# State-space scratch buffers in the form of the tiles, one transfer per unit for input, taps and output

## The chip, the cores and the metric

The kernel runs on one core of one Trainium2 chip. The metric is the time of one execution in microseconds of the device. The kernel before takes 2274.19 us, the median of three runs (2266.21 to 2277.70). Everything is float32; the large products are made of three matmuls each on a high and a low part.

## The reference

One layer of a hybrid encoder trunk: a projection whose columns go to a state-space branch (512 channels) and to chunked attention (8 heads of 64), both joined by one output projection, then a SwiGLU feed-forward. The state-space branch is the part that the change touches (SEQ 2048, 32 groups of 16 channels, 64 complex states per group):

```python
def s5_mixer(u, lam_re, lam_im, log_dt, b_re, b_im, c_re, c_im, d_skip, w_glu, b_glu):
    uf = u.astype(f32).reshape(bsz, seq, N_SSM_GROUPS, SSM_GROUP)
    ...
    lam_bar = jnp.exp(lam * dt)
    b_bar = ((lam_bar - 1.0) / lam)[..., None] * b_mat
    bu = jnp.einsum('bsgh,gph->bsgp', uf.astype(jnp.complex64), b_bar)
    ...
    _, states = lax.associative_scan(combine, (a, bu), axis=1)
    y = jnp.einsum('bsgp,ghp->bsgh', states, c_mat).real + d_skip.astype(f32) * uf
    y = jax.nn.gelu(y.reshape(bsz, seq, D_SSM))
    y = y * jax.nn.sigmoid(y @ w_glu.astype(f32) + b_glu.astype(f32))
    return y.astype(u.dtype)

def reference(...):
    h = rmsnorm(x, norm_mix_g[l]); proj = h @ w_in[l]
    ...
    mixed = jnp.concatenate([rmsnorm(y_ssm, ...), rmsnorm(y_att, ...)], axis=-1)
    x = x + mixed @ w_out[l]
    h2 = rmsnorm(x, norm_ffn_g[l])
    x = x + (jax.nn.silu(h2 @ w_gate[l]) * (h2 @ w_up[l])) @ w_down[l]
    return rmsnorm(x, norm_final_g)
```

## The kernel before

The program has five stretches, told here by the times of the profiled execution. From 0 to about 120 us `u_phase` makes the state-space input u for four blocks of 512 tokens, while `ssm_prologue` makes the taps and matrices of the scan and puts them into scratch buffers in memory. From 120 to about 700 us `att_phase` runs: 128 attention steps (4 blocks, 4 head pairs, 2 heads, 4 query blocks), each with scores, transposes and the product with v; between them stand units of other work, advanced step by step by class `Unit`: the projections of q, k and v of the next block (`qk_unit`, `v_unit`, `hT_unit`), and for the state-space branch eight times a `ssm_front` and a `ssm_back`. From about 700 to 960 us `mix_phase` makes the gated unit and the output projection; its first part is drawn into the last attention steps. Then come gate and up (960 to 1810 us) and down (to the end).

The state-space sequence is cut into pieces of L = 8 steps. A unit b handles GB = 4 groups: its input tile U has 128 partitions, which are 8 steps j times 16 channels c, and in each 4 groups times 256 pieces. So a row of the tile is 1024 numbers. Three scratch buffers in memory feed and empty these tiles:

- `S["u"]` is [512 channels, 4 blocks, 8 steps, 64]. `evac` (L484) writes it from the GpSimd queue, 16 times a [128, 512] tile, in rows of 2 KB. `ssm_front` reads it with eight DMAs per unit (L558 and L559, one for each step j, 16 partitions, runs of 64 numbers or 256 B).
- `S["kt"]` is [16, 32 groups, 2, 128]: zeros followed by the taps. `ssm_back` cuts eight shifted windows out of it, one DMA for each (L636 and L637, 16 partitions, runs of 512 B), into the tile Tm.
- `S["y"]` is [512 channels, 8 steps, 256]. `ssm_back` writes it with eight DMAs per unit (L650 and L651, runs of 1 KB). `fetch` (L1033) in the mix stage reads it back, twice 4 DMAs of 512 KB.

Channels of the group index and the channel within the group are in the order (c g) in u and in the order (g c) in y; the host lays the columns of the input projection out for the first.

All of these loads and the store of y go out on the queue of SyncE (SP), which issues in program order and waits in that order. The same queue carries the weights (`w<-wss`, 1 MB each), the bias rows of each head (`nba<-nbs` and `nbb<-nbs`, L549 and L550, one pair for each head), the copies of q between partition halves (`q2h`, `q2l`, L784 and L785), the keys (`ks`, L756 and L790) and the input of the next block (`xt` and `raw` from `in_xt`, L722). The DMAs of SP share eight completion semaphores in turn, so that each one waits for the one eight before it.

Which instruction stands where on a queue is decided by a scheduler when the program is built, except for TensorE, whose order is that of the text (`Ordered`, `PINA`), and a few marked instructions, among them the loads of unit 0 (the `b == 0` in `load`). GpSimd (POOL) also runs the scan of each unit (L592 to L604) and the moves of the carried states (`XG`, L626).

```python
SSM_F = 1 + GP + 7 + 7 + 3 + 4 + 1
SSM_B = 1 + GP + 1
SX = 4, 24, 35, 48, 61, 74, 87, 100
SY = 20, 36, 49, 62, 75, 88, 101, 114
```

SX and SY are the attention steps at which front and back of unit b begin.

Of the kernel before, what the change touches and what calls it, by code (L numbers as in the profile page):

```python
# [397 lines left out]
def u_phase(k, ident, S, aw):  # L398
# [3 lines left out]
    with ExitStack() as cx:  # L402
# [78 lines left out]
        def evac(b, f, ps):  # L481
            us = k.t(p3, "us", [P, L, NC // NSB])
            nc.vector.tensor_tensor(us[:], (jc if b else cj)(ps[:]), pbs[b], op=ALU.mult)
            nc.gpsimd.dma_start(S["u"][f * P : (f + 1) * P, b], us[:])  # L484

# [66 lines left out]


def ssm_front(k, p, psum, S, b, eng):

    nc = k.nc

    def load(out, in_):  # L558
        ins = nc.sync.dma_start(out, in_)  # L559
        if b == 0:  # L560
            k.tc.keep_in_program_order(ins)

    U = S["rsn"][:, : GB * NC].rearrange("p (g c) -> p g c", g=GB) if b and b % 2 == 0 else k.t(p, "U", [P, GB, NC])[:]
    k.U[b] = U
    for j in range(L):
        load(U[j * CH : (j + 1) * CH].rearrange("c g (n t) -> c g n t", n=NSB), S["u"].rearrange("(c g) n j t -> c g n j t", c=CH)[:, GB * b : GB * b + GB, :, j])
    bst = k.t(p, "Bst", [P, GB, P])
# [62 lines left out]
def ssm_back(k, p, psum, S, b):  # L630

    nc = k.nc
    F = GB * CH
    gs = slice(GB * b, GB * b + GB)
    tm = k.t(p, "Tm", [P, GB, P])
    for i in range(L):  # L636
        nc.sync.dma_start(tm[i * CH : (i + 1) * CH], S["kt"].rearrange("c g a m -> c g (a m)")[:, gs, P - CH * i : 2 * P - CH * i])  # L637
# [12 lines left out]
    for j in range(L):  # L650
        nc.sync.dma_start(S["y"][b * F : (b + 1) * F, j, :].rearrange("(g c) t -> c g t", c=CH), U[j * CH : (j + 1) * CH])  # L651
    yield


SSM_F = 1 + GP + 7 + 7 + 3 + 4 + 1
SSM_B = 1 + GP + 1
SX = 4, 24, 35, 48, 61, 74, 87, 100
SY = 20, 36, 49, 62, 75, 88, 101, 114
# [24 lines left out]
def att_phase(k, ident, S, aw, x0, roots):  # L683

    tc, nc, io, pfs = k.tc, k.nc, k.io, k.pfs
    with ExitStack() as cx:
# [253 lines left out]
        for sb in range(NSB):  # L940
# [7 lines left out]
            for gen, n, c in ((qk_unit(sb, 1), QK_N, 2), (qk_unit(sb, 2), QK_N, 3), (v_unit(sb, 1), V_N, 4), (qk_unit(sb, 3), QK_N, 5)):  # L948
                units.append(Unit(gen, n, g0 + C[c], g0 + C[c + 1], 2, light=LIGHT) if sb else Unit(gen, n + 1, C[c], C[c + 1], 4, light=LIGHT, mid=2))
        k.U = {}  # L950
        for b in range(NG // GB):
            units.append(Unit(ssm_front(k, sp, psum, S, b, k.ssm_eng), SSM_F, SX[b], SX[b] + 9, SX[b] - 2 if b == 0 else 2 if b == 1 else 5, light=SL))
            units.append(Unit(ssm_back(k, sp, psum, S, b), SSM_B, SY[b], SY[b] + 2, 6, light=SL))
# [27 lines left out]
def mix_phase(k, S, bank):  # L981
# [3 lines left out]
    with ExitStack() as cx:  # L985
# [44 lines left out]
        def fetch(sb):  # L1030
            yrs[0] = k.t(my, "yr", [P, 4, L, 128])
            for f in range(4):
                nc.sync.dma_start(yrs[0][:, f], S["y"][f * P : (f + 1) * P, :, sb * 64 : sb * 64 + 128])  # L1033

# [587 lines left out]
def block_kernel(tc, io, phases="pusamf"):  # L1622
# [3 lines left out]
    with ExitStack() as cx:  # L1626
# [4 lines left out]
        def pp():  # L1631
            return tc.tile_pool(name="psum", bufs=4, space=bass.MemoryType.PSUM, reuse_waits="tile")

        S = {
            "u": k.t(dram, "u", [DS, NSB, L, NC // NSB]), "y": k.t(dram, "y", [DS, L, NC]),
            "ya": k.t(dram, "ya_s", [NSB, DS, SB]), "x1": k.t(dram, "x1", [D, SEQ]),
# [3 lines left out]
            "hq": k.t(dram, "hq", [2, F2, 7, P, 512]), "wc": k.t(dram, "wc", [F2, 7, P, 512]), "wt": k.t(dram, "wt", [4, P, HALF]),  # L1640
            "kt": k.t(dram, "kts", [CH, NG, 2, P]),
        }
# [35 lines left out]
def layout(inputs):  # L1678
# [7 lines left out]
    def cols(v):  # L1686
        return np.ascontiguousarray(v.reshape(-1, P).T)

    def blocks(v, r, c):

        v = v.reshape(v.shape[0] // r, r // P, P, -1, c).transpose(0, 3, 2, 1, 4)
        return v.reshape(-1, P, r // P * c)

    x = a["x"][0].copy()
    x[SB:] = x[SB:].reshape(-1, SB // L, L, D).transpose(0, 2, 1, 3).reshape(-1, D)
    r = {
        "x": x, "xt": a["x"][0].T, "xp": x.T, "w_u": a["w_in"][0][:, :DS].reshape(D, NG, CH).transpose(0, 2, 1).reshape(D, DS),
        "w_qk": blocks(a["w_in"][0][:, DS : 3 * DS], D, P), "w_v": blocks(a["w_in"][0][:, 3 * DS :], D // 2, 256), "w_glu": a["ssm_w_glu"][0], "w_out": a["w_out"][0],
        "w_gate": blocks(a["w_gate"][0], D, P), "w_up": blocks(a["w_up"][0], D, P), "w_down": a["w_down"][0],
        "g_mix": cols(a["norm_mix_g"][0]), "g_ffn": cols(a["norm_ffn_g"][0]), "g_final": cols(a["norm_final_g"]),  # L1700
        "g_ssm": cols(a["norm_ssm_out_g"][0]), "g_att": cols(a["norm_att_out_g"][0]), "b_glu": cols(a["ssm_b_glu"][0]),
        "lam_re": pairs(a["ssm_lam_re"][0])[:, :, 0], "lam_im": pairs(a["ssm_lam_im"][0])[:, :, 0],
# [25 lines left out]
```

## Time and profile before

| what | value |
|---|---|
| median of three runs | 2274.19 us |
| the profiled execution, its own time | 2277.4 us |
| its span | 2275.6 us |
| TensorE matmul busy, share of the span | 2169.8 us, 95% |
| VectorE busy | 1542.7 us, 68% |
| ScalarE busy | 1002.5 us, 44% |
| GpSimd busy | 350.1 us, 15% |
| share of the 16 DMA engines taken by SP's queue | 54.6% |
| share taken by GpSimd's queue | 3.3% |
| mean granted TensorE clock | 0.978 |

The profile is one execution, followed instruction by instruction. Busy times of engines overlap, so they do not add up to the span. What matters for a change is the idle time of the engine that sets the end, here TensorE (PE), and what each of its waits was released by. The time of the profiled execution lies 3.2 us above the median.

### The profile page before, as it was taken

How to read it: one execution, taken by the hardware profiler on the slowest of the kernel's cores; microseconds unless marked ns; L12 is line 12 of the kernel's file. 1: busy time of each engine (PE TensorE's matmuls, PEld its weight loads, DVE VectorE, ACT ScalarE, POOL GpSimd, SP SyncE). 2: the span in 40 equal slices, each digit the busy share in tenths (PEclk: the TensorE clock that was granted, in tenths of full speed). 3: DMA queues.
4: the chain of work that ended last, by engine and by line, in shares of the span. 5: the costliest groups of instructions: out<-in, count | busy, mean ns of one | idle time of the engine just before them, and what ended most of it. 6: DMA issues, size and time to landing. Idle time of an engine off the chain costs nothing.

```text
span 2275.6 us, 30307 instructions
## 1 busy us (share of the span) xinstructions
PE 2169.8 (95%) x10632; PEld 1828.5 (80%) x10632; DVE 1542.7 (68%) x2695; ACT 1002.5 (44%) x1656; POOL 350.1 (15%) x827
## 2 busy tenths in 40 slices
PE   8989898999997899999999999999999999999997
PEld 6778787888986688878888887888888777888886
DVE  7757556555556756776767678666666477688776
ACT  6446555455557452343333335333333443353322
POOL 2246666646520000000000000000000010000000
PEclk9999999999998899999999999999999999999999
DMA  8778875766653535854555467655433395465652
GB/s 296 234 250 263 220 195 172 220 197 185 177 166 105 172 118 160 270 179 144 178 183 193 163 213 259 196 175 185 143 93 115 110 389 169 166 226 182 218 179 75
DMA packets 214874, 428.36 MB, mean 188 GB/s; under 512 B 38848, under 2 KB 61424, under 8 KB 207616
## 3 DMA queue, kind: packets, MB, share of 16 engines
q1 hardware_dynamic: 207072, 401.49, 54.6%
q0 software_dynamic: 7648, 24.92, 3.3%
q8 instruction: 84, 1.38, 0.2%
q14 instruction: 70, 0.57, 0.1%
HBM read 286.86 MB, written 129.00 MB: 183 GB/s over the span
## 4 chain that ended last, share of the span: by engine, by line
PE 77%; DMA 5%; DVE 5%; issue 4%; POOL 3%; ACT 2%; SPq 1%; DVEq 0%; ACTq 0%; POOLq 0%
PE X L76 20%; PE ps L76 17%; PE Y L76 10%; PE big L76 9%; PE pf L76 8%; PE W L76 5%; PE pj L76 3%; PE sc L76 2%; DMA acc<-x 2%; PE pt L79 2%; POOL X L595 1%; POOL X L594 1%; DMA lo<-hc 1%; POOL X L604 1%; POOL fx L603 1%
## 5 line engine op out<-in xcount | busy, mean ns | idle before, releaser
L76 PE MATMUL X<-hi,c 128*128 128x512 f32 x1408 | 451.3, 391 | 6.2 <-DVE c L153 5.5
L76 PE MATMUL ps<-hd,hd 128*128 128x512 f32 (+1 forms) x1968 | 429.7, 380 | 3.9 <-DVE hd L153 2.0
L76 PEld LDWEIGHTS ps<-hd,hd 128*128 128x128 f32 x1968 | 357.6, 189 | 74.6 <-DVE hd L153 2.7
L76 PEld LDWEIGHTS X<-hi,c 128*128 128x128 f32 x1408 | 265.4, 189 | 62.7 <-DVE c L153 6.4
L76 PE MATMUL X<-lo,c 128*128 128x512 f32 x704 | 274.9, 390 | 0.0
L153 ACT CAST hd<-hd 128x1536 fp32r<-128x1536 f32 (+1 forms) x106 | 147.3, 1393 | 234.6 <-DMA hd<-hq 148.1
L76 PE MATMUL Y<-hi,c 128*128 128x512 f32 x704 | 224.7, 390 | 2.1 <-DVE u L1407 2.1
L153 DVE TENSOR_TENSOR hd<-hd 128x1536 fp32r<-128x1536 f32 (+1 forms) x106 | 174.0, 1643 | 37.1 <-ACT hd L153 36.5
L153 DVE TENSOR_TENSOR c<-S,c 128x512 fp32r<-128x512 f32 x176 | 120.8, 687 | 98.9 <-ACT c L153 98.7
L1511 POOL DMA_DIRECT2D hd<-hq x7 | 5.3, 762 | 1169.5 <-PE X L76 1158.0
L1403 ACT COPY u<-X 128x512 f32<-128x512 f32 x132 | 77.3, 586 | 200.6 <-PE X L76 200.6
L76 PE MATMUL big<-m,woh 128*128 128x512 f32 x512 | 163.1, 400 | 0.0
L153 ACT CAST c<-S 128x512 fp32r<-128x512 f32 x176 | 109.3, 621 | 119.0 <-PE Y L76 61.8
L1545 DVE TENSOR_TENSOR acc<-acc,ps 128x512 f32<-128x512 f32 x196 | 130.3, 681 | 41.0 <-PE ps L76 40.7
L76 PEld LDWEIGHTS Y<-hi,c 128*128 128x128 f32 x704 | 132.3, 188 | 30.4 <-DVE u L1407 2.9
L76 PEld LDWEIGHTS X<-lo,c 128*128 128x128 f32 x704 | 132.8, 189 | 27.7
L76 PE MATMUL pf<-hi,w 128*128 128x512 f32 x416 | 150.7, 414 | 0.8 <-ACT hi L741 0.8
L153 ACT CAST c<-raw 128x512 fp32r<-128x512 f32 x132 | 82.2, 622 | 151.0 <-PE Y L76 64.3
L881 DVE TENSOR_TENSOR ptl<-pt,pth 128x640 fp32r<-128x640 f32 (+3 forms) x152 | 98.2, 646 | 66.6 <-ACT pth L880 64.8
L76 PE MATMUL Y<-lo,c 128*128 128x512 f32 x352 | 137.0, 389 | 0.0
L865 ACT ACTIVATE s<-s,mn 128x640 f32<-128x640 f32 (+4 forms) x128 | 97.9, 765 | 74.1 <-DVE mn L862 67.1
L880 ACT CAST pth<-pt 128x640 fp32r<-128x640 f32 (+3 forms) x152 | 83.6, 550 | 82.6 <-PE pt L79 77.6
(448 smaller groups left out, 4280.6 us busy)
## 6 DMA issues: line engine op xcount, KB each, us to landing
w<-wss SPq DMA_DIRECT2D x36, 1024.0 KB, 6.6
hq<-g SPq DMA_DIRECT2D x140, 256.0 KB, 2.1
hd<-hq SPq DMA_DIRECT2D x35, 768.0 KB, 4.5
hd<-wc SPq DMA_DIRECT2D x35, 768.0 KB, 5.9
raw<-in_w_gate SPq DMA_DIRECT2D x44, 512.0 KB, 3.7
raw<-in_w_up SPq DMA_DIRECT2D x44, 512.0 KB, 4.2
wc<-px SPq DMA_DIRECT2D x66, 256.0 KB, 2.9
wss<-w SPq DMA_DIRECT2D x12, 1024.0 KB, 5.8
```

Source lines behind the costliest of these rows:

```text
L76: return self.tc.keep_in_program_order(self.tc.nc.tensor.matmul(*a, **b))
L79: return self.tc.keep_in_program_order(self.tc.nc.tensor.transpose(*a, **b))
L153: return nc.scalar.copy(hi, raw), nc.vector.tensor_tensor(lo, raw, f32(hi), op=ALU.subtract)
L594: eng.tensor_tensor(dst, dst, t[:, :, :, :n], op=ALU.add)
L595: eng.tensor_tensor(dst, dst, t2[:, :, :, :n], op=ALU.add)
L603: eng.tensor_tensor(t, end[:, e].unsqueeze(3).to_broadcast([P, GP, n, 7]), pw, op=ALU.mult)
L604: eng.tensor_tensor(dst[:, c], dst[:, c], t, op=ALU.subtract if e == 1 and c == 0 else ALU.add)
L865: nc.scalar.activation(s[:, :nk], s[:, :nk], AF.Exp, bias=mn[:], scale=-1.0, accum_out=sums[sb, pr][:, hh, qp : qp + 1])
L880: nc.scalar.copy(pth[:, a:b, qp, :], pt[:, a:b, :])
L881: nc.vector.tensor_tensor(ptl[:, a:b, qp, :], pt[:, a:b, :], f32(pth[:, a:b, qp, :]), op=ALU.subtract)
L1403: nc.scalar.copy(u[:], ps[:])
L1545: V.tensor_tensor(a, a, ps[:], op=ALU.add)
```

## The change

The three buffers get the step j as their first index, so that (j c) is the tile's partition: `S["u"]` is [8, 512, 4, 64], `S["y"]` is [8, 512, 256], and there is a new buffer `S["tm"]`, [128, 32, 128], with the shifted windows of the taps for all groups. Channels are (c g) in y too; the host permutes the gate's matrix, its bias, the gains and the rows of the output projection to fit (`cg` in `layout`), which takes no time on the device.

```diff
@@ evac
-            nc.gpsimd.dma_start(S["u"][f * P : (f + 1) * P, b], us[:])
+            nc.gpsimd.dma_start(S["u"][:, f * P : (f + 1) * P, b].rearrange("j p t -> p j t"), us[:])
...
+def shifted_taps(k, S):
+
+    for i in range(L):
+        k.nc.sync.dma_start(S["tm"][i * CH : (i + 1) * CH], S["kt"].rearrange("c g a m -> c g (a m)")[:, :, P - CH * i : 2 * P - CH * i])
+        yield
...
@@ ssm_front
-    for j in range(L):
-        load(U[j * CH : (j + 1) * CH].rearrange("c g (n t) -> c g n t", n=NSB), S["u"].rearrange("(c g) n j t -> c g n j t", c=CH)[:, GB * b : GB * b + GB, :, j])
+    load(U.rearrange("p g t -> p (g t)"), S["u"].rearrange("j (c g) n t -> (j c) (g n t)", c=CH)[:, GB * NC * b : GB * NC * (b + 1)])
...
@@ ssm_back
-    for i in range(L):
-        nc.sync.dma_start(tm[i * CH : (i + 1) * CH], S["kt"].rearrange("c g a m -> c g (a m)")[:, gs, P - CH * i : 2 * P - CH * i])
+    nc.sync.dma_start(tm[:], S["tm"][:, gs])
...
-    for j in range(L):
-        nc.sync.dma_start(S["y"][b * F : (b + 1) * F, j, :].rearrange("(g c) t -> c g t", c=CH), U[j * CH : (j + 1) * CH])
+    nc.sync.dma_start(S["y"].rearrange("j (c g) t -> (j c) (g t)", c=CH)[:, GB * NC * b : GB * NC * (b + 1)], U.rearrange("p g t -> p (g t)"))
...
+ST = 2, 10
...
@@ att_phase
         k.U = {}
+        units.append(Unit(shifted_taps(k, S), L, *ST))
...
@@ fetch
-                nc.sync.dma_start(yrs[0][:, f], S["y"][f * P : (f + 1) * P, :, sb * 64 : sb * 64 + 128])
+                nc.sync.dma_start(yrs[0][:, f], S["y"][:, f * P : (f + 1) * P, sb * 64 : sb * 64 + 128].rearrange("j p t -> p j t"))
...
@@ block_kernel
-            "u": k.t(dram, "u", [DS, NSB, L, NC // NSB]), "y": k.t(dram, "y", [DS, L, NC]),
+            "u": k.t(dram, "u", [L, DS, NSB, NC // NSB]), "y": k.t(dram, "y", [L, DS, NC]),
...
-            "kt": k.t(dram, "kts", [CH, NG, 2, P]),
+            "kt": k.t(dram, "kts", [CH, NG, 2, P]), "tm": k.t(dram, "tms", [P, NG, P]),
```

Counted over the program, on SP's queue 64 loads of U become 8 (rows of 4 KB in place of 256 B), 64 loads of Tm become 8 (rows of 2 KB in place of 512 B) after 8 copies from `kt` to `tm` within memory, and 64 stores of y become 8 (rows of 4 KB in place of 1 KB). On GpSimd's queue the 16 stores of u stay 16, but each is now 1024 pieces of 256 B in place of 128 rows of 2 KB. The order of TensorE's instructions stays as it was. The scheduler sets SP, VectorE and ScalarE anew between the start of the attention and its end; from the mix stage on the order is that of before. Three places of SP's queue follow.

The first is SP at the start of the attention, before (the names: `hi0x`, `lo0x`, `hi1x`, `lo1x` are copies of the first head pair's q from one partition half to the other, `wss<-w` stores of split weights, 1 MB each):

```order
L637 DMA Tm_2321<-kts_78 16x4x128 x8
L639 DMA Vm_2330<-vs_71 128x4x128
L784 DMA hi0x_1383<-hi0x_1383 64x512
L784 DMA hi1x_1386<-hi1x_1386 64x512
L713 DMA wss_74<-w_1537 128x2048
L785 DMA lo0x_1384<-lo0x_1384 64x512
```

and in the changed kernel:

```order
L557 DMA tms_79<-kts_78 512x128
L566 DMA U_1708<-u_64 128x1024
L566 DMA Bst_1710<-bsts_70 128x512
L557 DMA tms_79<-kts_78 512x128
L788 DMA hi0x_1384<-hi0x_1384 64x512
L789 DMA lo0x_1385<-lo0x_1385 64x512
```

The loads of Tm and Vm left this place; the load of unit 0's U and Bst, which stood behind the copies of q, now stands ahead of them, and the store of 1 MB that stood between hi0x and lo0x now follows later.

The second is SP where unit 0 ends and unit 1 begins (`raw` and `xt` hold the input of block 1), before:

```order
L651 DMA y_65<-U_1705 16x4x256
L707 DMA w_2623<-wss_74 128x2048
L784 DMA q2h_2512<-q2h_2512 64x512
L785 DMA q2l_2513<-q2l_2513 64x512
L784 DMA q2h_2515<-q2h_2515 64x512
L785 DMA q2l_2516<-q2l_2516 64x512
L651 DMA y_65<-U_1705 16x4x256 x7
L722 DMA raw_2675<-in_xt 128x2x512
L559 DMA Bst_2686<-bsts_70 128x512
L559 DMA U_2677<-u_64 16x16x64 x8
```

and now:

```order
L654 DMA y_65<-U_1708 128x1024
L788 DMA q2h_2507<-q2h_2507 64x512
L789 DMA q2l_2508<-q2l_2508 64x512
L788 DMA q2h_2510<-q2h_2510 64x512
L789 DMA q2l_2511<-q2l_2511 64x512
L711 DMA w_2618<-wss_74 128x2048
L726 DMA xt_2659<-in_xt 128x512
L726 DMA raw_2661<-in_xt 128x2x512
L726 DMA raw_2663<-in_xt 128x2x512
L566 DMA U_2665<-u_64 128x1024
```

The store of y is one row ahead of the copies of q, and seven stores between them and U are gone; one `xt` and the first of the two `raw` loads, which stood earlier in the queue before, now stand directly ahead of U.

The third is SP in the second block, with the bias rows of the next head (`nbb`), before:

```order
L756 DMA k_1000_4591<-ks_68 128x512
L637 DMA Tm_4617<-kts_78 16x4x128 x8
L639 DMA Vm_4626<-vs_71 128x4x128
L559 DMA rsn_92<-u_64 16x16x64
L756 DMA k_1003_4594<-ks_68 128x512
L559 DMA rsn_92<-u_64 16x16x64 x7
L559 DMA Bst_4636<-bsts_70 128x512
L549 DMA nbb_1549<-nbs_69 64x576
L550 DMA nbb_1549<-nbs_69 64x576
```

and now, first the loads of the same unit, which stand earlier:

```order
L641 DMA Tm_4556<-tms_79 128x512
L643 DMA Vm_4558<-vs_71 128x4x128
L654 DMA y_65<-rsn_93 128x1024
L566 DMA rsn_93<-u_64 128x1024
L711 DMA w_4354<-wss_74 128x2048
```

and then the stretch with the bias rows:

```order
L760 DMA k_1001_4530<-ks_68 128x512
L726 DMA xt_6074<-in_xt 128x512
L549 DMA nbb_1550<-nbs_69 64x576
L550 DMA nbb_1550<-nbs_69 64x576
L711 DMA w_4718<-wss_74 128x2048
L794 DMA ks_68<-k_921_4221 128x512
L794 DMA ks_68<-k_924_4224 128x512
L726 DMA raw_6183<-in_xt 128x2x512
L726 DMA xt_6181<-in_xt 128x512
L726 DMA raw_6185<-in_xt 128x2x512
L711 DMA w_4720<-wss_74 128x2048
L760 DMA k_1004_4533<-ks_68 128x512
```

The bias rows stood behind the second key load `k_1003`, which waits for TensorE, and behind sixteen small loads; now they stand ahead of the second key load (`k_1004`). In exchange the load of U (`rsn<-u`) follows the store of y with nothing between, and has to wait for it to land, since both use the same tile.

More of the change, by code (lines that the diff above doesn't have):

```diff
@@ L632, in ssm_back @@
     nc = k.nc
-    F = GB * CH
     gs = slice(GB * b, GB * b + GB)
     tm = k.t(p, "Tm", [P, GB, P])
-    for i in range(L):
-        nc.sync.dma_start(tm[i * CH : (i + 1) * CH], S["kt"].rearrange("c g a m -> c g (a m)")[:, gs, P - CH * i : 2 * P - CH * i])
+    nc.sync.dma_start(tm[:], S["tm"][:, gs])
     vm = k.t(p, "Vm", [P, GB, P])
@@ L1692, in blocks, with cg @@
         return v.reshape(-1, P, r // P * c)
+    def cg(v):
+        return v.reshape(NG, CH, -1).transpose(1, 0, 2).reshape(v.shape)
     x = a["x"][0].copy()
@@ L1696, in layout @@
     r = {
-        "x": x, "xt": a["x"][0].T, "xp": x.T, "w_u": a["w_in"][0][:, :DS].reshape(D, NG, CH).transpose(0, 2, 1).reshape(D, DS),
-        "w_qk": blocks(a["w_in"][0][:, DS : 3 * DS], D, P), "w_v": blocks(a["w_in"][0][:, 3 * DS :], D // 2, 256), "w_glu": a["ssm_w_glu"][0], "w_out": a["w_out"][0],
+        "x": x, "xt": a["x"][0].T, "xp": x.T, "w_u": cg(a["w_in"][0][:, :DS].T).T,
+        "w_qk": blocks(a["w_in"][0][:, DS : 3 * DS], D, P), "w_v": blocks(a["w_in"][0][:, 3 * DS :], D // 2, 256), "w_glu": cg(cg(a["ssm_w_glu"][0]).T).T, "w_out": np.concatenate([cg(a["w_out"][0][:DS]), a["w_out"][0][DS:]]),
         "w_gate": blocks(a["w_gate"][0], D, P), "w_up": blocks(a["w_up"][0], D, P), "w_down": a["w_down"][0],
         "g_mix": cols(a["norm_mix_g"][0]), "g_ffn": cols(a["norm_ffn_g"][0]), "g_final": cols(a["norm_final_g"]),
-        "g_ssm": cols(a["norm_ssm_out_g"][0]), "g_att": cols(a["norm_att_out_g"][0]), "b_glu": cols(a["ssm_b_glu"][0]),
+        "g_ssm": cols(cg(a["norm_ssm_out_g"][0])), "g_att": cols(a["norm_att_out_g"][0]), "b_glu": cols(cg(a["ssm_b_glu"][0])),
         "lam_re": pairs(a["ssm_lam_re"][0])[:, :, 0], "lam_im": pairs(a["ssm_lam_im"][0])[:, :, 0],
```

## The prediction

> **What bounds the kernel now.** I read the page first, then the busy time by stage, then the chain of waits and the waits of TensorE (PE) in the stage that the change touches, and last SP's queue there. The page:
>
> ```profile
> PE 2169.8 (95%) x10632; PEld 1828.5 (80%) x10632; DVE 1542.7 (68%) x2695; ACT 1002.5 (44%) x1656; POOL 350.1 (15%) x827
> ```
>
> PE sets the end; 106 us of the span are its idle time. The stages, with PE's busy time first, the granted clock, the DMA share and GB/s last:
>
> ```profile
> 120.00:700.00 580.00, 527.96 (x3174) 472.06 (x3172) 332.22 (x627) 320.41 (x671) 308.27 (x752) 0.95 0.70 204
> 960.00:1810.00 850.00, 843.21 (x3707) 696.50 (x3707) 581.45 (x910) 327.77 (x567) 2.77 (x4) 1.00 0.51 166
> ```
>
> In the attention (120 to 700) PE idles for 580.00 − 527.96 = 52 us, in the far longer gate-and-up stage for 7. Only the first of these stages holds state-space transfers, so the 52 us are nearly all that they can have a part in. PE's waits there, with the idle time and its releaser at the end of each row:
>
> ```profile
> 136.45 0.48 PE L76 MATMUL sc<-hi2x,lo0x 128*128 128x128 f32 x1 [3.11 <-DMA lo0x<-lo0x]
> 240.77 3.75 PE L76 MATMUL pj<-U,Bst 128*128 128x256 f32 x8 [4.20 <-DMA ks<-k]
> 377.30 0.42 PE L76 MATMUL sc<-k,q2h 128*128 128x320 f32 x1 [1.31 <-DVE k L788]
> 386.52 0.80 PE L76 MATMUL pf<-lo,w 128*128 128x512 f32 x1 [3.58 <-DVE lo L742]
> 406.79 0.38 PE L76 MATMUL sc<-k,q2h 128*128 128x320 f32 x1 [3.75 <-DVE mn L862]
> 466.11 0.43 PE L76 MATMUL sc<-k,q2h 128*128 128x320 f32 x1 [2.64 <-DVE mn L862]
> 543.05 3.45 PE pj L76 x16
> ```
>
> The last row, from the chain, is the price of such products without a wait: 3.45 / 16 = 0.22 us each. The eight behind the wait at 240.77 took 3.75 in place of 1.73, so this wait cost about 2 us more than its 4.20. What VectorE's `mn` and `lo` were late for, the chain tells:
>
> ```profile
> 131.67 4.74 DMA lo0x<-lo0x
> 370.59 5.38 DMA nba<-nbs
> 401.26 4.41 DMA nbb<-nbs
> 461.63 3.37 DMA nba<-nbs
> ```
>
> Beside the copy of q, `lo0x`, they are the bias rows of the next head, landing late. Why, SP's queue shows (start, time, and the number of DMAs):
>
> ```profile
> 129.81 0.49 SPq L784 DMA_DIRECT2D hi0x<-hi0x  x1
> 131.67 0.46 SPq L785 DMA_DIRECT2D lo0x<-lo0x  x1
> 202.96 1.07 SPq L722 DMA_DIRECT2D raw<-in_xt  x1
> 226.87 4.19 SPq L651 DMA_DIRECT2D y<-U  x7
> 231.10 0.43 SPq L722 DMA_DIRECT2D raw<-in_xt  x1
> 233.14 4.58 SPq L559 DMA_DIRECT2D U<-u  x8
> 396.48 0.34 SPq L756 DMA_DIRECT2D k<-ks  x1
> 396.86 3.38 SPq L559 DMA_DIRECT2D rsn<-u  x7
> 400.77 0.45 SPq L549 DMA_DIRECT2D nbb<-nbs  x1
> 456.13 4.95 SPq L559 DMA_DIRECT2D U<-u  x8
> 461.12 0.47 SPq L549 DMA_DIRECT2D nba<-nbs  x1
> ```
>
> So it is the order and the length of SP's queue, not the bytes, through which state-space transfers reach PE: a group of eight stands ahead of what PE needs at 233, 397 and 456.
>
> **What the change takes from SP.** An issue costs, by tile (min, median, max in ns):
>
> ```profile
> L559 SPq DMA_DIRECT2D U<-u x40: 302/448/1363, 139.3 to 575.3; - x40
> L637 SPq DMA_DIRECT2D Tm<-kts x64: 303/426/1531, 114.3 to 631.6; - x64
> ```
>
> 192 issues become 32 (8 each for U, Tm, y and the copies of the taps), so 160 × about 0.43 = 69 us of SP's time go. SP is not what ends the program; this is a cover, and it is worth only what it moves ahead of PE's waits. Hence the sum goes wait by wait.
>
> **Term 1, start of the attention.** lo0x goes out 1.9 us behind hi0x with a store of 1 MB between, and lands 4.7 us later. In the changed order it follows hi0x at once, the store behind it; hi0x landed in 2.2. So up to 2.5 of the 3.11 us go, more only if it issues sooner: −3.1 at best. But U's load now stands ahead of hi0x and waits for the last stores of u, which become 1024 pieces of 256 B. Their prices:
>
> ```profile
> hi0x<-hi0x SPq DMA_DIRECT2D x1, 128.0 KB, 2.2
> u<-us POOLq DMA_DIRECT2D x16, 256.0 KB, 4.3
> vs<-v POOLq DMA_DIRECT2D x16, 144.0 KB, 3.9
> 116.46 0.57 POOL L484 DMA_DIRECT2D u<-us  x1 [2.39 <-DVE us L483]
> 119.55 0.54 POOL L484 DMA_DIRECT2D u<-us  x1 [0.49 <-DVE us L483]
> 139.26 7.72 SPq L559 DMA_DIRECT2D U<-u  x8
> U<-u SPq DMA_DIRECT2D x40, 64.0 KB, 4.0
> L484 POOL DMA_DIRECT2D u<-us x16: 539/544/642, 45.3 to 119.5; - x16
> L365 POOL DMA_DIRECT2D vs<-v x16: 631/633/662, 49.5 to 91.0; - x16
> ```
>
> The last columns of the DMA rows are the median us to landing. No store in pieces of 256 B is in the trace. From below: `vs` has 256 pieces of 576 B on the same queue, `u` 128; issue 0.633 against 0.544, so 0.7 ns a piece, 0.63 + 0.54 = 1.2 us for 1024, and no longer landing (3.9 against 4.3). Then the last store issues at about 120, lands at 125, and U, Bst and a copy of taps (three issues, 1.3 us) leave SP free at 126.3, 3.5 us before hi0x is ready at 129.81: hidden by that. From above: U's load, 2048 pieces of 256 B, took 7.72 + 4.0 = 11.7 us, or 5.7 ns a piece; four stores of 1024 in a row would be 23 us from 116.5, hi0x 11 us late, and PE with it. A store from GpSimd is nearest to the rows of its own queue, so I take the lower one: **−2**, bounds −3.1 to +11.
>
> [...]
>
> **Term 2, unit 1.** One y store goes out where the first of eight did, and U no longer waits behind seven more. U would then be there before PE is, and the 4.20 plus 2 of slow products go: −6.2 at best. Against it: both loads of raw, of which one went at 202.96, now stand ahead of U and go at about 228, with a weight of 1 MB and one xt; 1 + 1 + 0.25 + 0.5 MB at the stage's 204 GB/s are 13 us, so the last may land at 240 with five pairs of VectorE operations behind it: PE may wait there up to 3. I take **−3**, bounds −6.2 to +3, on the side of the gain, since the wait for U is seen in the trace and one for raw is not.
>
> **Term 3, 377 to 387.** The bias rows at 370 stood behind four copies of q and a weight; now they stand ahead of those, and both raw loads of block 2, which went right behind them, stand many rows earlier. 1.31 + 3.58 = 4.9 hang on this. **−4**, bounds −4.9 to 0.
>
> **Term 4, 406.79.** The bias rows at 400.77 stood behind a key load that waited for PE till 396.48 and behind seven U loads. Both are no longer ahead: **−3** of 3.75, bounds −3.75 to 0. **Term 5, 466.11**, the same with U's eight at 456: **−2** of 2.64, bounds −2.64 to 0.
>
> **Term 6, a wait that is new.** For five of the later units U's load stands one to four rows behind the y store that frees its tile. It must land first, as one transfer of 512 KB: between the 64 KB stores and the nearest row of that size,
>
> ```profile
> y<-U SPq DMA_DIRECT2D x40, 64.0 KB, 2.2
> yr<-y SPq DMA_DIRECT2D x8, 512.0 KB, 6.1
> ```
>
> so 2 to 6 us, about 4, in which SP issues nothing: 5 × 4 = 20 us, a third of what it won. Behind it stand weights, y of the attention, keys and bias rows. The bias rows are asked for two steps ahead of their use, a step is 580 / 128 = 4.5 us, and they took 3.4 to 5.4 to land, so some 4 us of a hold are covered. Most of it is hidden then: **+3**, bounds 0 to +20, and all 20 if that cover is gone.
>
> **Term 7, traffic.** Eight copies within memory add 2 MB read and 2 MB written between 105 and 195 us, and the small rows of U move from 64 loads to 16 stores. PE does not wait for bytes there: **+0.5**, bounds 0 to +3. On GpSimd the stores of the scan's input matrices move ahead of the products of powers, and each store of u takes 0.6 us longer; what covers both is the idle time before the first scan:
>
> ```profile
> 165.46 0.47 POOL L592 TENSOR_TENSOR st<-X,a 128x128 f32<-128x128 f32 x1 [26.13 <-ACT X L578]
> ```
>
> With 26 us free they cost nothing; without, they would cost the 2.5 us of four stores. The mix stage, whose order is that of before, is costed at nothing too: the rows of its loads of y keep their 512 B.
>
> Sum: −2 − 3 − 4 − 3 − 2 + 3 + 0.5 = **−10.5 us**. The profiled execution's own time, 2277.4 (span 2275.6 and 1.8 around it), becomes 2266.9. It stood 3.2 above the median of the runs shown, 2274.2, so I state **2264** for the median.
>
> **The rivals.**
> - *Given back* (0.22): SP is early, but the next thing in the chain of each wait, VectorE's order or the q and k of the next head, takes its place. For it, the longest group of PE's waits in this stage has no DMA in it, and the scheduler has reordered VectorE and ScalarE throughout:
>
> ```profile
> PE pt L79 <- DVE ptl L881: 11.0, 6, 6.1
> ```
>
> Against it, five waits have a DMA behind them by name. Terms 3 to 5 would be zero: 2264 + 9 = 2273.
> - *SP held by y's landing* (0.21, the slower side): term 6 at its upper end, 20 us, because bias rows and copies of q behind the held U are due when they issue; terms 3 to 5 then are lost as well, as they hang on the same rows. 2264 + 17 + 9 = 2290. It is slower than before from a term 6 of about 5 with those terms lost, or 13.5 with them kept. Against it: SP's own time falls by 69.
> - *Small stores* (0.08): a piece of 256 B costs the store what it costs U's load, 5.7 ns, and the last four land 23 us after 116.5; term 1 is +11, the rest as forecast: 2264 + 13 = 2277. Against it, `vs` lands no later than `u` with twice the pieces.
> - *Everything at its best* (0.12): −3.1 − 6.2 − 4.9 − 3.75 − 2.64, with terms 6 and 7 nil, is −20.6: 2254.
> - *Forecast* (0.37), 2257 to 2270.
>
> **How the numbers follow.** A measurement here can tell about 0.5%, 11 us, from no change: below 2263 is faster, above 2285.5 slower. Of the forecast 0.27 lies below and 0.10 within; with the best case faster has 0.39. Within: 0.10, 0.20 of the first rival, 0.06 of the third, 0.36. Slower: 0.21 and what is left over, 0.04, together 0.25. The range 2248 to 2289 leaves out the lower part of the best case and the upper half of the slower one, about 0.15; the forecast's own range is 2257 to 2270.
>
> **What would show it.** PE's wait for lo0x below 1 us; U of unit 1 landed before PE's products with it, and no slow ones behind; the bias rows at 370, 401 and 461 issued 8 us or more before their use, and no wait on `mn` above 1 us at those steps; SP's waits for DMAs of y near 20 us in all, with no PE wait behind them. The forecast is wrong if hi0x issues after 131 with U ahead of it, if PE's idle time from 120 to 700 is still near 52 us, or if new waits of PE for `q2h`, `k` or `mn` stand behind a U that waited for y.

## The result and the profile after

The changed kernel takes 2261.85 us (median of eight runs, 2258.59 to 2267.91) against 2274.38 for the kernel before (eight runs beside it, 2266.21 to 2277.70): a ratio of 0.9943, 95% interval 0.993 to 0.9957, or 12.5 us less. (The ratios here and below are those on record; they are not quotients of the medians and differ from these by up to 0.1%.) Forecast were 2264, 10.5 us less. The size came out; the sum behind it did not, as the profile shows. The execution profiled took 2267.91 us, the longest of the eight, as that of before with 2277.4 was long among its own.

The first line of the page after, then two stretches by windows (PE's busy time first, the granted clock, the DMA share and GB/s last):

```profile
PE 2165.6 (96%) x10632; PEld 1825.8 (81%) x10632; DVE 1542.4 (68%) x2695; ACT 1003.3 (44%) x1656; POOL 351.2 (15%) x827
```

```profile
120.00:700.00 580.00, 530.61 (x3221) 475.80 (x3219) 339.58 (x640) 331.60 (x686) 307.19 (x755) 0.97 0.67 211
...
122.90:688.25 565.35, 521.16 (x3173) 467.71 (x3172) 331.64 (x627) 320.40 (x671) 304.70 (x752) 0.97 0.68 214
```

The first of the two is the window of the prediction. It holds 580.00 − 530.61 = 49.4 us of idle time against 52.0 and seems to say that little happened. But the work has moved: TensorE's order is the same in both kernels, so the same matmul can be found in both traces, and what stood at 120 us before stands at 122.9 now. At 700 PE waits for a matmul that starts at 703.56; now that one starts at 691.81, so the same place is 688.25. Over the same work (the second row; 3174 matmuls before, 3173 now) idle time falls from 52.0 to 44.2 and busy time from 527.96 to 521.16, at a granted clock of 0.97 in place of 0.95. The difference of the two executions, by the same matmuls:

| stretch | change, us | of it |
|---|---|---|
| start to the 561st matmul (120.55 before, 123.43 now) | +2.9 | the stage that makes u |
| from there to the end of the attention (the matmul at 703.56 before, 691.81 now) | −14.6 | −7.8 idle, −6.8 busy |
| mix, gate and up, down, to the last matmul | +2.8 | comes around the start of gate and up (the lead is 12.2 us at 924 and 8.9 at 995), where no transfer of the change is; its cause stays open |

TensorE's waits of over 1.3 us between 125 and 540 us, from the timeline (idle time and its releaser at the end):

```profile
138.05 0.44 PE L76 MATMUL sc<-hi2x,hi0x 128*128 128x128 f32 x1 [6.32 <-DMA hi0x<-hi0x]
...
194.74 0.55 PE L76 MATMUL sc<-k,q2h 128*128 128x256 f32 x1 [5.84 <-DVE mn L866]
...
238.77 0.30 PE L76 MATMUL sc<-k,q2h 128*128 128x128 f32 x1 [2.20 <-issue]
...
245.65 3.35 PE L76 MATMUL pj<-U,Bst 128*128 128x256 f32 x8 [4.04 <-DMA Bst<-bsts]
...
289.43 1.33 PE L79 MATMUL pt<-ident,s 128*128 128x128 f32 x5 [3.12 <-DVE ptl L885]
...
385.25 0.64 PE L76 MATMUL sc<-k,q2h 128*128 128x320 f32 x1 [4.08 <-DVE k L792]
...
401.14 0.77 PE L79 MATMUL pt<-ident,s 128*128 128x128 f32 x5 [1.31 <-DVE ptl L885]
```

Those at 238.77 and 289.43 have a counterpart before (2.20 at 232.70, and 3.05 at 292.06 a few products on). After 401 us none is left: the waits on `mn` at 406.79 and 466.11 are gone, and so are two that the prediction did not price, of before (a third, 2.31 for `ptl` at 210.41, fell to 1.0):

```profile
492.82 0.41 PE L76 MATMUL sc<-k,q2h 128*128 128x320 f32 x1 [1.59 <-DVE mn L862]
...
537.13 1.22 PE L76 MATMUL pj<-rsn,Bst 128*128 128x256 f32 x4 [3.46 <-DVE ya L905]
```

But two are new, 1.31 at 401.14 and the longest but one, 5.84 at 194.74. SP's queue ahead of it, after the change:

```profile
127.64 0.33 SPq L566 DMA_DIRECT2D U<-u  x1
128.87 0.32 SPq L566 DMA_DIRECT2D Bst<-bsts  x1
129.24 0.57 SPq L557 DMA_DIRECT2D tms<-kts  x1
132.69 0.50 SPq L788 DMA_DIRECT2D hi0x<-hi0x  x1
134.31 0.48 SPq L789 DMA_DIRECT2D lo0x<-lo0x  x1
...
174.37 0.50 SPq L557 DMA_DIRECT2D tms<-kts  x1
174.92 0.63 SPq L717 DMA_DIRECT2D wss<-w  x1
175.60 2.14 SPq L557 DMA_DIRECT2D tms<-kts  x2
180.83 0.48 SPq L788 DMA_DIRECT2D q2h<-q2h  x1
...
186.53 0.48 SPq L549 DMA_DIRECT2D nbb<-nbs  x1
...
236.61 0.71 SPq L566 DMA_DIRECT2D U<-u  x1
237.37 0.45 SPq L566 DMA_DIRECT2D Bst<-bsts  x1
```

and before the change, for the same bias rows:

```profile
174.64 0.45 SPq L549 DMA_DIRECT2D nbb<-nbs  x1
```

The copies of the taps (`tms<-kts`) and the copies of q, which wait for ScalarE, stand ahead of the bias rows now: these go out at 186.5, 12 us later. The three copies just ahead took 2.6 of the 12 (0.50 + 2.14); from 177.7 to 185.4 the queue stood at those of q. PE is done at 188.9, and the first of the rows' two loads lands at 191.6. Yet the wait for the scores' `mn` lasts until 194.74, since VectorE has a new order too. Its rows after, and the one for the same scores before:

```profile
192.02 2.36 DVE L153 TENSOR_TENSOR w<-raw,w 128x1024 fp32r<-128x1024 f32 x2 [0.27 <-ACT w L153]
194.30 0.28 DVE L866 CUSTOM_DVE_ANT_0 s<-sc,nbb 128x128 f32<-128x128 f32 x1
```

```profile
187.22 0.28 DVE L862 CUSTOM_DVE_ANT_0 s<-sc,nbb 128x128 f32<-128x128 f32 x1
```

The two operations on the weights `w` stand right ahead of the scores now; before, they ran at 177.54 and 180.75. Their loads have moved behind the copies as well: they go out at 185.42 now, and went at 165.39 and 174.16. So what the wait ends with is not the landing of the bias rows but VectorE's order, in which work on weights that came late stands ahead of the scores. Why the scheduler chose this order is not shown.

### The profile page after: what moved, and what is told of

It is laid out like the page before. It is cut to its first block, busy times and chain, and to the rows that moved or that the text cites. A ratio compares the mean times of both kernels' runs of the same rounds, so it can differ in the third digit from the quotient of the medians.

```text
span 2266.1 us, 30134 instructions
## 1 busy us (share of the span) xinstructions
PE 2165.6 (96%) x10632; PEld 1825.8 (81%) x10632; DVE 1542.4 (68%) x2695; ACT 1003.3 (44%) x1656; POOL 351.2 (15%) x827
## 4 chain that ended last, share of the span: by engine, by line
PE 78%; DMA 7%; DVE 6%; ACT 3%; issue 2%; SPq 0%; DVEq 0%; ACTq 0%
PE X L76 20%; PE ps L76 17%; PE Y L76 10%; PE pf L76 10%; PE big L76 6%; PE W L76 5%; PE pj L76 4%; PE pt L79 2%; PE sc L76 2%; DMA acc<-x 2%; DMA lo<-hc 1%; DMA xt<-in_xt 1%; DVE lo L153 1%; DMA hc<-gh 1%; DVE ptl L885 1%
```

## The experiments

**First set: eight issues again, and each buffer alone.** Theory of the queue: a group of eight issues on SP stands ahead of what PE needs, and one issue does not. Rivals: the form (larger rows), and the order (VectorE and ScalarE dealt out anew by the scheduler).

The changed buffers with each transfer in eight by the step j; here the load of U, Tm and y likewise:

```diff
-    load(U.rearrange("p g t -> p (g t)"), S["u"].rearrange("j (c g) n t -> (j c) (g n t)", c=CH)[:, GB * NC * b : GB * NC * (b + 1)])
+    for j in range(L):
+        load(U[j * CH : (j + 1) * CH].rearrange("c g t -> c (g t)"), S["u"][j].rearrange("(c g) n t -> c (g n t)", c=CH)[:, GB * NC * b : GB * NC * (b + 1)])
```

> The changed buffers, but each transfer of a unit cut into eight by the step j again: U, Tm and y in rows of 4 KB, 2 KB and 4 KB, with 192 issues on SP as before the change and the 8 copies of the taps beside them. Theory of the queue (what PE gains comes from the issues that no longer stand ahead of the bias rows and of U): nothing of the gain is left, 2272 to 2280 us, and PE waits for mn or U again at the places that follow a group of eight. Rival, form (the larger rows are what helps, since the DMA engines are done sooner): 2258 to 2266 us. Rival, order (the scheduler has dealt out VectorE's and ScalarE's work anew, and any edit does that): the time can lie anywhere from 2255 to 2285 us, and the waits that are left are on ptl, mn or k with no DMA late behind them.

Measured: 2282.59 against 2272.86 (ratio 1.0036, 1.0023 to 1.005): slower, and above the 2272 to 2280 of the queue's theory. The rows were 4, 2 and 4 KB, and the gain was gone with a loss beside it, so the form is not what helps. SP's queue and PE behind it at the place of term 4:

```profile
407.55 3.21 SPq L566 DMA_DIRECT2D rsn<-u  x7
...
411.27 0.45 SPq L549 DMA_DIRECT2D nbb<-nbs  x1
```

```profile
417.42 0.60 PE L76 MATMUL sc<-k,q2h 128*128 128x320 f32 x1 [3.70 <-DVE mn L869]
```

It is the picture of the kernel before at 396 to 407, with its wait of 3.75. Now each buffer alone (the diffs are the parts of the change that name it; y with the host's permutation).

> Only the buffer of u takes the tile's form: u stores in pieces of 256 B, one U load for each unit; taps and y as before. Theory of the queue: U's eight stood ahead of the bias rows at 396 and 456 us and U itself was late in unit 1, so this part carries most: 2264 to 2269 us (6 to 10 us faster), and the waits of PE on mn at 406.79 and 466.11 are gone. Rival, form: U's rows of 256 B are the smallest that go, so the same size of gain, but with the waits elsewhere. Rival, order: no fixed sign. Rival, small stores: unit 0's start waits for the last stores of u, PE waits 5 us or more longer at the first scores than in the kernel before.

> Only the taps: 8 copies within memory, then one Tm load for each unit; u and y as before. Theory of the queue: the loads of Tm stand ahead of bias rows only where U's do (397 us), 64 issues or 27 us of SP's time go but little of it ahead of a wait of PE: 2271 to 2276 us. Rival, form: the rows go from 512 B to 2 KB, with 4 MB more of traffic for the copies: 2270 to 2280 us. Rival, order: as far from the kernel before as the others are, up to 10 us in either direction.

> Only y: one store for each unit, 512 KB in rows of 4 KB, and the host's permutation of the gate's channels that goes with it; u and taps as before. Theory of the queue: U of unit 1 stands behind one store in place of eight, which takes some of the wait of 4.20 us at 240.77; but U's eight loads now wait behind the landing of the whole store: 2269 to 2276 us. Rival, form: 1 KB to 4 KB rows of 4 MB in all: no change, 2272 to 2277 us. Rival, order: up to 10 us in either direction.

| kernel | median, us | before beside it | ratio, 95% interval |
|---|---|---|---|
| u alone | 2257.04 | 2272.86 | 0.993 (0.9918 to 0.9943) |
| y alone | 2257.08 | 2272.86 | 0.9928 (0.9913 to 0.9943) |
| taps alone | 2277.75 | 2272.86 | 1.0021 (1.0009 to 1.0034) |

All three missed the times that the queue's theory gave them (taps alone lies in the range of the form's rival); that the waits on `mn` at 406.79 and 466.11 go with u alone, but for 0.6 us, came as expected. u and y alone each win 16 us by the medians, against 12.5 for the whole change, whose interval theirs overlap; the taps alone lose. In u alone and in y alone three waits of PE are gone but for 0.6 us, those of before at 386.52, 466.11 and 537.13: 3.58 + 2.64 + 3.46 = 9.7, so some 9 us. y alone keeps U's eight loads, six of them still right ahead of the bias rows (442.68 to 446.6), and its 16 us are not the gain that the queue's theory had forecast for it. PE's waits with the taps alone:

```profile
190.60 0.55 PE L76 MATMUL sc<-k,q2h 128*128 128x256 f32 x1 [5.84 <-DVE mn L869]
...
247.14 3.61 PE L76 MATMUL pj<-U,Bst 128*128 128x256 f32 x8 [10.48 <-DMA ks<-k]
```

The wait of 5.84 is there in the three kernels with the copies so far, and in neither of the others. So the copies bring it. It is 5.84 each time, while the first of the bias rows lands 2.7 to 3.0 us after its start, so that it is not this landing that ends it.

**Second set: the copies, and the small stores.**

u and y without the taps: `shifted_taps` and `S["tm"]` are left out of the change, and Tm is loaded as before.

> The buffers of u and y in the tiles' form, the taps loaded as before by eight DMAs for each unit; the copies within memory are gone. Theory of the copies (on SP's queue they push the bias rows for the scores at 194.74 back, where PE waits 5.84 us for mn in the three runs that have them, and the load of unit 1's U or Bst, where taps alone waits 10.48 in place of 4.20): neither wait is there, and the time is 2250 to 2257 us, at least 5 us below the whole change. Rival, the gains of u and of y are one and the same (each leaves unit 1's and the second block's waits, each alone is at 2257): 2256 to 2260, no better than either alone. Rival, order: any value from 2250 to 2275.

Measured: 2257.35 against 2273.85 (0.9926, 0.99 to 0.9951). Neither 5.84 nor a wait for U of unit 1 is there, as the theory had it; but the time is no better than that of u or y alone, as the first rival had it. The gains do not add, and one reason is in the traces: the 9 us of waits that each alone removes can go only once.

The copies issued by GpSimd:

```diff
-        k.nc.sync.dma_start(S["tm"][i * CH : (i + 1) * CH], S["kt"].rearrange("c g a m -> c g (a m)")[:, :, P - CH * i : 2 * P - CH * i])
+        k.nc.gpsimd.dma_start(S["tm"][i * CH : (i + 1) * CH], S["kt"].rearrange("c g a m -> c g (a m)")[:, :, P - CH * i : 2 * P - CH * i])
```

> The whole change, but the eight copies of the taps are issued by GpSimd in place of SP. Theory of the copies' place in SP's queue: the bias rows issue near 175 us again, PE's wait of 5.84 at 194.74 is gone or below 1 us, and the time falls to 2250 to 2258 us. Rival, the copies' traffic (4 MB between 105 and 180 us make other loads late): the wait stays, 2260 to 2265 us. Rival on GpSimd: the copies stand ahead of the last stores of u and of the products of powers, unit 0's scan begins later and XG with it, PE waits 2 us or more for Vm's products of unit 0: 2262 to 2270 us.

Measured: 2271.27 (0.9989, 0.9974 to 1.0004), a miss for all three. The wait at 194.74 went, but others came, one of them longer:

```profile
139.50 0.48 PE L76 MATMUL sc<-hi2x,lo0x 128*128 128x128 f32 x1 [4.69 <-DMA lo0x<-lo0x]
...
153.15 0.58 PE L76 MATMUL sc<-hi2x,hi0x 128*128 128x256 f32 x1 [8.41 <-DVE mn L866]
```

What `mn` was late for, the chain of waits of that kernel says:

```profile
143.02 9.01 DMA xt<-in_xt
```

With SP free of the copies, the scheduler put the input of block 1 that early, and on VectorE its first operation stands ahead of `mn`, waiting 9 us for the bytes.

The copies later, still on SP:

```diff
-ST = 2, 10
+ST = 9, 13
```

> The whole change with the copies of the taps begun at attention step 9 in place of 2 (ST = 9, 13), still on SP. Five of the eight then stand behind the bias rows for the scores at 194.74 in place of none. Theory of the copies' place: the wait there falls below 3 us, while the copies now stand ahead of the next bias rows, which may be late in their turn by up to 3: 2255 to 2262 us. Rival, traffic: no change from the whole change beyond 2 us, 2260 to 2264.

Measured: 2257.66 (0.994, 0.9919 to 0.996). The median is 4 us below that of the whole change, but the ratios, 0.994 and 0.9943, do not tell the two apart. The trace does: the first of the bias rows is out at 171.77, ahead of four of the eight copies, and no wait on `mn` stands at the former 194.74; one is left at unit 1. SP's queue of that kernel, and PE:

```profile
171.77 0.47 SPq L549 DMA_DIRECT2D nbb<-nbs  x1
...
182.47 0.75 SPq L557 DMA_DIRECT2D tms<-kts  x1
184.92 1.20 SPq L557 DMA_DIRECT2D tms<-kts  x2
```

```profile
237.24 3.75 PE L76 MATMUL pj<-U,Bst 128*128 128x256 f32 x8 [5.40 <-DMA Bst<-bsts]
```

So the wait of 5.84 hangs on the copies' place in the program's order, not on their bytes; SP's queue and VectorE's order change together here, and this run does not part them.

The kernel before with padded rows of u; the load of U takes the first half of each row:

```diff
-            nc.gpsimd.dma_start(S["u"][f * P : (f + 1) * P, b], us[:])
+            nc.gpsimd.dma_start(S["u"][f * P : (f + 1) * P, b, :, : NC // NSB], us[:])
...
-            "u": k.t(dram, "u", [DS, NSB, L, NC // NSB]),
+            "u": k.t(dram, "u", [DS, NSB, L, 2 * NC // NSB]),
```

> The kernel before with u's rows of 64 numbers padded to 128 in memory, so that its 16 stores are 1024 pieces of 256 B each as in the changed kernel, while U is loaded in the same pieces of 256 B, eight loads for each unit. It prices the small stores alone. If they are what makes PE 2.3 to 4.2 us later by 100 us in the three runs that have them (and in none of the three that have not): lag of 2 to 4 us at 100 us, 2275 to 2280 us in all, GpSimd's issue 0.885 us in place of 0.544 and landing near 5. Rival, chance between single executions: lag within 1 us, 2271 to 2275. Rival of the prediction, small stores at 5.7 ns a piece: hi0x 11 us late, 2285.

Measured: 2278.15 against 2273.85 (1.0018, 1.0003 to 1.0033): slower by 4.3, the first theory's value, though by little more than the interval. GpSimd's issue of them, from the view of the tile in the kernel after (min, median, max in ns), and the median us to landing from its DMA issues:

```profile
L484 POOL DMA_DIRECT2D u<-us x16: 885/888/978, 46.7 to 122.4; - x16
```

```profile
u<-us POOLq DMA_DIRECT2D x16, 256.0 KB, 5.0
```

The start of the 561st matmul, in us, in all traces (for the expectation's "lag by 100 us"; the offset does not change between 100 and 120):

| u in stores of 2 KB | start | u in pieces of 256 B | start |
|---|---|---|---|
| before | 120.55 | after | 123.43 |
| y alone | 120.22 | u alone | 122.36 |
| taps alone | 119.52 | eight issues | 124.43 |
| taps and y | 119.92 | u and y | 123.61 |
| taps late, y | 119.03 | copies by GpSimd | 121.83 |
| before, prefetch 7 | 118.66 | copies later | 122.41 |
| | | padded u | 121.41 |
| | | after, prefetch 7 | 122.76 |

All eight with small stores are later than all six without; the means differ by 122.78 − 119.65 = 3.1 us. The padded kernel itself lags least, 0.9 us behind the kernel before and 1.8 behind the mean of the six, below the 2 to 4 expected. No single wait carries it: it is spread over short waits for the input's loads, so that these loads suffer under the stores is argued, not shown.

**Third set: the single U, and the order as a rival.**

Taps and y alone (`evac`, the load of U and `S["u"]` as before), once with the copies where the change has them and once with ST = 9, 13:

> Taps and y in the tiles' form, u as before (2 KB stores, eight loads of U for each unit). If the parts add up in the places where PE waits: y's 16 us less, taps' 4 us more, so 2260 to 2263 us, with the wait of 5.84 us for mn at the first block's scores still there and no lag by 100 us. Rival, the single load of U is what the whole change lives on: 2268 to 2275 us, with PE's wait on mn at 406.79 (eight loads of U ahead of the bias rows) still there. Rival, order: anywhere between 2250 and 2280.

Measured: 2269.96 against 2272.95 (0.9987, 0.9972 to 1.0002), the rival's time: without the single load of U most of the gain is lost, though the wait at 406.79 fell to 1.30. The parts do not add.

> The same with the copies of the taps begun at attention step 9 (ST = 9, 13), where they stand behind the bias rows for the first block's scores. Theory of the copies' place: the wait of 5.84 us is gone, and the time is 4 us or more below the kernel of the run before it, 2252 to 2258 us, without the small stores' 3 us. Rival, the copies only move the wait to the next bias rows or to U of unit 1: within 2 us of the run before it.

Measured: 2262.69 (0.9958, 0.9943 to 0.9972): the copies' place was worth 7 us here, and the wait of 5.84 is gone again; the time is above the 2252 to 2258 expected, with a wait of 7.37 for U of unit 1 that grew from 5.13.

One number in the kernel before:

```diff
-            units.append(Unit(ssm_back(k, sp, psum, S, b), SSM_B, SY[b], SY[b] + 2, 6, light=SL))
+            units.append(Unit(ssm_back(k, sp, psum, S, b), SSM_B, SY[b], SY[b] + 2, 7, light=SL))
```

> The kernel before with one number changed: the loads of Tm and Vm of a unit may begin seven attention steps ahead in place of six. No transfer is added, taken or altered, but the scheduler deals out SP, VectorE and ScalarE anew from about 270 us on. It prices the rival of order, that any edit moves the time as far as these do. Theory of the queue: the eight loads stand a little elsewhere, the groups of eight ahead of the bias rows remain: 2268 to 2279 us, within 5 us of the kernel before. Rival, order: 8 us or more in either direction.

Measured: 2286.69 against 2272.95 (1.0064, 1.0051 to 1.0077): 14 us slower, for one number and no transfer more or less. That is the rival's size. But the trace puts it on SP's queue:

```profile
321.75 0.95 SPq L707 DMA_DIRECT2D w<-wss  x2
322.75 12.51 SPq L559 DMA_DIRECT2D U<-u  x8
...
461.42 11.22 SPq L559 DMA_DIRECT2D U<-u  x8
472.84 0.47 SPq L549 DMA_DIRECT2D nba<-nbs  x1
```

```profile
329.34 0.59 PE L76 MATMUL pf<-w,hi0x 128*128 128x256 f32 x2 [4.63 <-DMA w<-wss]
334.98 0.80 PE L76 MATMUL pf<-w,hi 128*128 128x256 f32 x2 [2.90 <-DMA w<-wss]
...
478.11 0.61 PE L76 MATMUL sc<-k,q2h 128*128 128x320 f32 x1 [5.77 <-DVE mn L862]
```

Eight loads of Tm moved ahead of weights, and the eight of U, which stood ahead of the bias rows before too (4.95 us at 456.13), take 11 us there now, right behind two weights. So here the order did its harm through the queue, where a group of eight stands ahead of what PE needs. That is not all that an order does: the waits of 5.84 above and of 3.46 at 537.13 end with VectorE, which had other work ahead, and not with a DMA. The last run makes the same edit in the changed kernel, to see whether single issues are proof against it.

> The whole change with the same one number changed as in the run before (Tm and Vm seven attention steps ahead in place of six), which cost the kernel before 14 us. Theory of the queue: that cost was a group of eight loads of Tm and of U moved ahead of the weights and bias rows; where each is one issue a move of it holds nothing up, so the time stays within 4 us of the whole change, 2258 to 2266 us, and PE waits neither for w nor 5 us for mn at the former places. Rival, order of VectorE and ScalarE: the new deal costs here as much as there, 2270 to 2280 us.

Measured: 2263.02 against 2273.19 (0.9957, 0.9941 to 0.9973), 1 us from the whole change, where the same number cost the kernel before 14. No wait for `w` of 1.3 us or more, and none on `mn` but the 5.84 at 194.5.

The lowest medians are those of u alone, y alone, u and y, and the whole change with later copies, all at 2257 to 2258; their differences are below what these runs can tell, and their intervals overlap that of the whole change.

## Why the prediction was right, and where it was not

| term | forecast | in the traces |
|---|---|---|
| 1, start of the attention | −2 | −0.8: 4.04 + 3.11 became 6.32 |
| 2, unit 1 | −3 | −0.6: 4.20 + 3.75 became 4.04 + 3.35 |
| 3, 377 to 387 | −4 | −0.8: 1.31 + 3.58 became 4.08 |
| 4, 406.79 | −3 | −2.4: 3.75 gone, 1.31 new at 401.14 |
| 5, 466.11 | −2 | −2.6: gone |
| 6, hold of SP for y | +3 | 0 |
| 7, traffic | +0.5 | +5.8 of wait that the copies brought, and some 3 of late start, put to the small stores |
| waits at 210.41, 492.82 and 537.13 | not in the sum | −6.4 |
| clock after waits | some 2, in unit 1 | −6.8 in the stage |

**Term 1.** lo0x was right behind hi0x as foreseen and PE's wait for it is gone. But hi0x itself, with U, Bst and a copy in front of it, landed late, in the chain of the kernel after:

```profile
132.69 5.22 DMA hi0x<-hi0x
...
237.37 8.15 DMA Bst<-bsts
```

5.22 us against 2.2; that the bytes ahead slowed it is argued. U's load did wait for the last stores of u, till 127.6, and that was hidden, as the lower bound had it; the Small-stores rival's +11 did not come. By the letter one of the prediction's marks of being wrong was met, hi0x at 132.69, after 131, with U ahead of it; but before it went at 129.81, and the stage's start is later by just those 2.9 us, so U did not hold it. What the rival named may have cost elsewhere, in the stage that makes u.

**Term 2.** The step "U would then be there before PE is" failed. The second row just shown is why: U went out at 236.61 behind `xt` and both `raw`, Bst behind it, and Bst took 8.15 us. The danger that the term named, raw ahead of U, was real, and with it came a transfer that it did not count. Without the copies (u and y) PE does not wait there.

**Term 3** is the *Given back* rival in small, and its reading of the trace before was wrong for the larger part: the bias rows had landed there by 376.0, and `lo` was late behind VectorE's own work on `xt` and `raw` from 380.2 to 385.0. `lo` is no longer late, since block 2's input came early; but then VectorE works on that input ahead of the key, on which PE waits 4.08:

```profile
380.49 1.08 DVE L744 SCALAR_TENSOR_TENSOR xt<-xt,g_mix,rsn 128x512 f32<-128x512 f32 x1
381.49 2.99 DVE L746 TENSOR_TENSOR lo<-raw,hi 128x512 fp32r<-128x512 f32 x2
384.51 0.68 DVE L792 TENSOR_TENSOR k<-pf,k 64x512 fp32r<-64x512 f32 x1
```

**Terms 4 and 5** held, mechanism and size: the bias rows that went out at 400.77 and 461.12 now do so at 379.16 and 442.10, and VectorE no longer waits for them.

**Term 6** was over-sized. SP's waits for y, summed from its waits after the change:

```profile
SPq L566 <- DMA y<-U: 7.5, 3, 4.2
SPq L566 <- DMA y<-rsn: 4.2, 1, 4.2
```

11.7 us in four waits, where 20 in five were expected, with no PE wait of 1.3 us or more behind any. The hold is real, its cover was enough, and the *SP held* rival is out.

**Term 7 is the step that failed.** "PE does not wait for bytes there" is true and beside the point: the term priced the copies by their traffic and the 192 issues that go by their number, and did not place the eight new issues in the program's order, as the terms before it had done for U and the bias rows. With them there the bias rows and the weights' loads go out 11 to 20 us later, and VectorE takes up `w` ahead of the scores; PE waits 5.84 us, plus what the clock takes (below). The wait is in all five kernels that issue the copies from SP at this place and in none of the others. For VectorE's order the sum had no term at all; the *Given back* rival had named it. The late start, put to the small stores, which were costed at nothing outside term 1, took some 3 us more.

What made up for both are three waits for which no term was written, and the clock. These waits are not the mechanism of terms 4 and 5. At 537.13 the `ya` that PE waited for could have run from 527.5, when ScalarE was done with its input, but stood on VectorE behind the next block's input and the key till 536.30; now VectorE does it first. At 210.41 too VectorE had weights and input ahead, and at 492.82 a `raw` that came late. So the order of VectorE won time at these places and lost it at 194.74, and neither was forecast. That the total came out near was luck, since errors of both signs met: the attention gave 7.8 us of idle time, the clock 6.8 on top, the start took 2.9 back and the stages behind 2.8. Together this is 8.9 between the two executions profiled, and 12.5 between the medians. Of the marks that the prediction set, "idle time from 120 to 700 still near 52" would have read wrong at 49.4, since the window did not move with the work.

Open in part: why u and y, each worth 16, are worth no more together. Some 9 us of idle time are the same three waits in both. In the kernel with both, PE waits 4.09 for the key at the place of term 3, and starts 3 us late; y alone has 1.79 there and no late start, some 5 us more. Why these three waits go in both is not shown.

## What to carry to other kernels

On a queue that issues in order, price a transfer by what stands behind it, not by its bytes: a group of eight small issues is worth as much as what it keeps waiting (in the kernel with eight issues, 3.21 us of SP for seven of them ahead of the bias rows, and 3.70 of PE's wait behind), and new copies that shorten later loads have a place in the queue too (with them moved later the wait of 5.84 was gone). Where a scheduler deals the engines' work out anew, look also at what the releasing engine did between the landing and the end of the wait: it may have been busy with something else. In the one case tried, single issues made the time insensitive to a changed prefetch distance (1 us against 14); to who issues the copies it stayed sensitive (2271 with GpSimd, 2262 with SP). When two executions are compared by stage, cut both at the same instruction, not at the same microsecond.

## What the runs showed of the hardware

A wait can cost more than its idle time. The kernel before around its wait of 2.64, and the kernel after around its wait of 5.84 (the granted clock is the third number from the end):

```profile
463.50:466.10 2.60, 0.00 (x0) 0.02 (x1) 0.83 (x2) 0.04 (x1) 0.00 (x0) 1.00 0.94 291
466.30:469.70 3.40, 3.40 (x13) 3.06 (x13) 0.83 (x2) 2.08 (x5) 0.00 (x0) 0.50 0.89 228
469.80:473.20 3.40, 3.40 (x20) 3.01 (x19) 2.31 (x4) 1.08 (x3) 0.00 (x0) 1.00 0.90 284
```

```profile
193.90:200.70 6.80, 5.96 (x27) 5.99 (x28) 1.97 (x7) 1.72 (x6) 6.12 (x14) 0.50 1.00 383
```

After the wait PE runs at half its clock for 3.4 us in the one case and 6.8 in the other (the second begins within the idle time). At the 5.84 the same matmuls fall back against the kernel before by 6.0 us with the wait, and by 2.3 more until the clock is back. In the stage, over the same work, PE's busy time at half clock falls from 36.1 us to 22.3; half of the difference, an estimate of what the clock took less, is 6.9, against the 6.8 us of busy time which the stage won. A stretch at half clock does not follow every wait: after the 3.75 us at 406.79 in the kernel before, the granted clock stays at 1.00. In that trace the stretches at half clock between 380 and 540 us start at 384.39, 466.31 and 537.99 and last 6.8, 3.4 and 3.4 us: one begins within the wait of 3.58, the others 0.2 and 0.9 us behind the ends of those of 2.64 and 3.46. What decides at which wait one comes is not shown.

A store by GpSimd in 1024 pieces of 256 B took 0.888 us to issue against 0.544 in 128 rows of 2 KB, and 5.0 to land against 4.3: the 0.7 us more are 0.8 ns for each of the 896 pieces more, far below the 5.7 ns a piece that the loads of U had suggested. If the 3 us by which u's stage ends later are the stores', the third rival had the sign right, and not the size.
